# Rotary turn of the shared key by two row transfers and a column of signs in place of a product, and a planner that counts changes of the array's shape

## The chip, the core and the metric

The kernel runs on one core of a Trainium2 chip. A core has five engines with instruction streams of their own: TensorE (PE, the products, with a separate stream of weight loads, PEld), VectorE (DVE), ScalarE (ACT), GpSimd (POOL) and SyncE (SP, which here issues transfers). Streams wait for each other through semaphores only. The metric is the device time of one execution in microseconds (us), lower is better: the median of three executions before is 956.06 us (955.11 to 957.71).

## What is computed

One layer of a diffusion backbone over 512 latent tokens and 256 context tokens of 1024 features: modulated norms, then in parallel a latent attention with 16 heads and a two-way Mamba-2 scan with 16 heads, a joint output projection, and a gated MLP with a convolution on its gate. Cut to what the change touches, which is the rotary part of the key, shared by all heads:

```
cq_x, ckv_x, kr_x, z_x, xbc_x, dt_x = in_split(modulate(rms_norm(x, ...), ...) @ w_in)

def rotate_half_axial(x):                 # x: (..., 32)
    def rh(t):
        a, b = jnp.split(t, 2, axis=-1)
        return jnp.concatenate([-b, a], axis=-1)
    xr, xc = jnp.split(x, 2, axis=-1)
    return jnp.concatenate([rh(xr), rh(xc)], axis=-1)

def apply_rope(x, cos, sin):
    return x * cos + rotate_half_axial(x) * sin

k_rope_x = apply_rope(kr_x, cos, sin)     # 512 tokens x 32; context keys are not turned
s = (einsum("bqhd,bkhd->bhqk", q_nope, k_nope) + einsum("bqhr,bkr->bhqk", q_rope, k_rope)) * SCALE
```

The kernel holds the 32 features on partitions 32 to 63, reordered so that the two quarters a turn swaps are rows 32 to 47 and rows 48 to 63; the sine table is negative on rows below 64. Every product of weights and activations is made of rounded fp32r halves: a value is split into a high part (ACT copy, L597) and a low part (DVE subtraction, L598), and three products of halves replace one.

## The kernel before

The program is written once as plain code, and a planner then sets the order. build() (from L566) issues some 8,000 instructions in the order of the source. plan() collects them, prices each one (price), finds their dependences, and replays them on a model of the engines (Graph.schedule): each engine takes, of what is ready, the instruction of the lowest rank. refined() then changes ranks at random, with a fixed seed, 1200 times, and keeps a change that the model does not call longer. The orders that come out are the instruction streams. So a change of prices, of the rule for extra time (1340 ns in TABLE for each change of the ACT table) or of the instructions themselves makes the search draw another order for all engines.

Stages, by the profile's clock: modulation from 12 to 60 us, the input projections from there to about 245 us (products L862, 8 input blocks by three half products; the convolution on DVE L892, its smooth gate L903), with the key made on the way at L988; the scan's products; attention scores from 255 to 505 us; output projection; MLP with up projection to 840 us; and the down projection (L1671), which multiplies 2 by 2 blocks by a scheme with seven products, so that DVE makes sums of blocks (L1664, L1680, L1570) and splits them before a product can run.

Shared places set much of the waiting. The eight PSUM banks are cut into areas by hand: in the attention, two areas "sc" of 768 columns for score tiles and two banks "t" for transposed tiles. A score tile (L1309, six products) is reduced on DVE (L1311), exponentiated on ACT (L1313), which frees its area; the result is transposed by six products (L1325) into the two "t" banks, which ACT (L597) and DVE (L598) empty into halves. The weighted sums are L1337.

The rotary turn stands at L997 to L1003, behind the fused key product:

```
    pr = pget("b")
    mm(pr[:64, :S], lhsT=C("rot")[:64, :64], rhs=kd[:, :S], start=True, stop=True)
    kc, ks = t2(64, S), t2(64, S)
    V.tensor_tensor(out=kc[32:64], in0=kd[32:64, :S], in1=C("cos")[32:64], op=ALU.mult)
    V.tensor_tensor(out=ks[32:64], in0=pr[32:64, :S], in1=C("sin")[32:64], op=ALU.mult)
    pfree(pr)
    V.tensor_tensor(out=kd[32:64, :S], in0=kc[32:64], in1=ks[32:64], op=ALU.add)
```

The 64 by 64 matrix "rot" of zeros, ones and minus ones is a part of the constants that SP loads (L589, 64 KB); another transfer brings the tables "cos" and "sin" (512 KB). The product is plain fp32 and shows as two records. A changed line L997 of the new kernel is another one than L997 here: the new kernel's numbers are lower by 2 from L65 on, and by 3 from about L868 on.

Of the kernel before, what the change touches and what calls it, by code (L numbers as in the profile page):

```python
# [15 lines left out]
ALU = mybir.AluOpType  # L16
# [3 lines left out]
P = 128  # L20
# [26 lines left out]
_o = 0  # L47
for _n, _w in (("id", 128), ("sel", 32), ("rot", 128), ("trif", 128), ("trib", 128), ("cos", 512), ("sin", 512)):
    CST[_n] = (_o, _w)
    _o += _w  # L50
# [3 lines left out]
def constants():  # L54
    c = np.zeros((P, NCST), np.float32)

    def put(name, a):
        o, w = CST[name]
        c[: a.shape[0], o : o + w] = a

    i = np.arange(P)
    put("id", np.eye(P))
    put("trif", (i[:, None] <= i[None, :]))
    put("trib", (i[:, None] >= i[None, :]))
    rot = np.zeros((64, P))  # L65
    for m in range(16):
        rot[48 + m, 32 + m] = 1.0
        rot[32 + m, 48 + m] = -1.0
    put("rot", rot)
    t = np.arange(S)  # L70
    inv = np.float32(10000.0) ** (-np.arange(0, 16, 2, dtype=np.float32) / np.float32(16))
    ar = (t // GRID_W).astype(np.float32)[:, None] * inv
    ac = (t % GRID_W).astype(np.float32)[:, None] * inv
    ang = np.concatenate([ar, ac], -1).astype(np.float64)
    put("cos", np.tile(np.cos(ang).T, (8, 1)))
    put("sin", np.where(i[:, None] < 64, -1, 1) * np.tile(np.sin(ang).T, (8, 1)))
    put("sel", np.tile(np.eye(32), (2, 1)))
    return c
# [77 lines left out]

TABLE, TICK, WARM, BEGIN = 1340, 10240 / 3, 3060, 570


def price(x):  # L160
# [10 lines left out]
    if e == "PE":  # L171
        if ops[1][2].dtype == mybir.dt.float32r:
            return size(ops[1]) / (2.4 if size(ops[1]) >= 256 else 1.2) + (13 if ops[1][1][0][1] > 64 else 100)
        return max(107, size(ops[1]) / 1.2) if x.is_transpose else max(213, size(ops[1]) / 0.6)
# [35 lines left out]
def table(x):  # L210

    return {AF.Tanh: 0, AF.Exp: 0, AF.Ln: 1, AF.Gelu: 2, AF.Sqrt: 3}.get(getattr(x, "func", None))

# [99 lines left out]
class Graph:  # L313
# [39 lines left out]
    def schedule(self, rank, look=0.06, back=False):  # L353
# [7 lines left out]
        later, now, due = [[] for _ in ENGINES], [[] for _ in ENGINES], [never] * len(ENGINES)  # L361
        ticks, held, port, queue, flying = {}, 0, 0.0, 0.0, []
        push, pop = heapq.heappush, heapq.heappop
# [14 lines left out]
        for _ in range(n):  # L378
# [18 lines left out]
            c, d = cost[i], dma[i]  # L397
            if not back and tables[i] not in (None, held):
                held, t = tables[i], t + TABLE
            if shared[i]:  # L400
# [165 lines left out]
def build(nc, tc, ctx, a, out, dbg=None, places=None):  # L566
# [10 lines left out]
    def c_(shape, name, dt=F32):  # L577
        return cp.tile(list(shape), dt, name=name, tag=name, bufs=1)
# [9 lines left out]
    def load(dst, src, q=None):  # L588
        (q or nc.sync).dma_start(out=dst, in_=src)  # L589
# [68 lines left out]
    cs, csc = t4(), t4()  # L658
    cst = c_([P, P + 32 + P], "cst")
    prm = c_([P, NPRM], "prm")  # L660
    load(cst[:, : P + 32], a["cst"][:, : P + 32], nc.scalar)
    load(prm, a["prm"])
# [206 lines left out]

    load(cst[:, P + 32 :], a["cst"][:, P + 32 : 2 * P + 32])  # L870
    for name, w, get in (("trif", 256, t2), ("cos", 1024, t4)):
# [124 lines left out]

    pr = pget("b")  # L997
    mm(pr[:64, :S], lhsT=C("rot")[:64, :64], rhs=kd[:, :S], start=True, stop=True)
    kc, ks = t2(64, S), t2(64, S)
    V.tensor_tensor(out=kc[32:64], in0=kd[32:64, :S], in1=C("cos")[32:64], op=ALU.mult)  # L1000
    V.tensor_tensor(out=ks[32:64], in0=pr[32:64, :S], in1=C("sin")[32:64], op=ALU.mult)
    pfree(pr)
    V.tensor_tensor(out=kd[32:64, :S], in0=kc[32:64], in1=ks[32:64], op=ALU.add)  # L1003
# [848 lines left out]
```

## Time and profile before

| what | value |
|---|---|
| median of three executions | 956.06 us |
| profiled execution, its own time | 954.86 us |
| span of the profiled execution, first to last instruction | 953.1 us |
| granted TensorE clock, mean | 0.992 |
| score tiles: 64 reductions L1311 | 60.7 us of DVE |
| half splits: DVE L598, all forms | 461 instructions |

The profile is one execution. Its windows give, for a stretch of time, how long each engine was busy and with how many instructions; its waits give which instruction's end released an engine; its timeline gives starts and lengths one by one, neighbours of one kind together. The ends of products are modelled and they overlap, so what a product costs on TensorE is best read from the distance of starts. 954.86 us lies 1.20 us under the median and inside the range of the three.

### The profile page before, as it was taken

The page shows a single profiled execution, that of the slowest core. Times are in us where ns is not written, and L with a number is a line of the kernel's source. Part 1 is how long each engine was busy: PE and PEld are TensorE (multiplying, and loading weights), DVE is VectorE, ACT ScalarE, POOL GpSimd, SP SyncE. Part 2 cuts the span into 40 slices and gives each one's busy share as a digit, 9 for nine tenths or more (in the row PEclk, how much of TensorE's full clock was granted, in tenths as well). Part 3 has the DMA queues.
Part 4 walks back from the last instruction along what each step waited for, and adds up shares of the span by engine and source line. Part 5 has one row for each costly group of instructions (what it writes and reads, how often), then busy time and mean ns, then how long its engine had stood idle before and what let it go on. Part 6 is the DMA issues. An engine that isn't in the chain of part 4 may idle for free.

```text
span 953.1 us, 14651 instructions
## 1 busy us (share of the span) xinstructions
PE 938.1 (98%) x5116; PEld 802.4 (84%) x5116; DVE 749.7 (79%) x1378; ACT 526.1 (55%) x1038; POOL 246.2 (26%) x258
## 2 busy tenths in 40 slices
PE   8999999999999999999999999999999999999996
PEld 8888888888888988889898888988888888878785
DVE  6999868897989999877899986832544744579998
ACT  4465337544877878688895236633313322347674
POOL 0001001766669466522111100000000063240021
PEclk9999999999999999999999999999999999999999
DMA  9953103012432434244849874413343232856784
GB/s 346 335 179 127 50 1 100 1 51 78 103 67 62 114 101 110 55 104 99 253 168 326 277 245 153 177 67 133 133 177 132 89 111 69 206 112 196 235 286 145
DMA packets 54586, 137.52 MB, mean 144 GB/s; under 512 B 8033, under 2 KB 11121, under 8 KB 54513
## 3 DMA queue, kind: packets, MB, share of 16 engines
q1 hardware_dynamic: 52128, 132.03, 43.0%
q0 software_dynamic: 1584, 2.88, 1.9%
q10 hardware_dynamic: 800, 1.68, 0.6%
q8 instruction: 40, 0.66, 0.3%
q14 instruction: 34, 0.27, 0.1%
HBM read 114.50 MB, written 6.34 MB: 127 GB/s over the span
## 4 chain that ended last, share of the span: by engine, by line
PE 88%; DVE 7%; ACT 2%; issue 1%; DMA 1%; POOL 0%; SPq 0%; DVEq 0%; ACTq 0%
PE banks L862 43%; PE banks L1437 9%; PE banks L1309 6%; PE banks L1671 6%; PE banks L794 5%; PE banks L1337 4%; PE banks L1325 4%; DVE block L598 3%; PE banks L1235 2%; PE banks L1134 2%; DVE block L1664 1%; PE banks L706 1%; PE banks L1180 1%; PE banks L1172 1%; ACT block L597 1%
## 5 line engine op out<-in xcount | busy, mean ns | idle before, releaser
L862 PE MATMUL banks<-block,block 128*128 128x512 f32 (+1 forms) x2132 | 450.8, 362 | 0.4 <-DVE block L1258 0.3
L862 PEld LDWEIGHTS banks<-block,block 128*128 128x128 f32 x2132 | 359.4, 189 | 61.9 <-issue 1.6
L597 ACT ACTIVATE block<-block 128x512 fp32r<-128x512 f32 (+4 forms) x329 | 208.5, 670 | 150.7 <-DVE block L696 30.3
L598 DVE TENSOR_TENSOR block<-block,block 128x512 fp32r<-128x512 f32 (+3 forms) x305 | 236.3, 809 | 63.4 <-ACT block L597 34.4
L1671 PE MATMUL banks<-block,block 128*128 128x512 f32 x462 | 111.4, 396 | 2.8 <-DVE block L1680 2.1
L1671 PEld LDWEIGHTS banks<-block,block 128*128 128x128 f32 x462 | 87.1, 190 | 23.9 <-DVE block L1680 2.6
L1309 PE MATMUL banks<-block,block 128*128 128x512 f32 (+1 forms) x384 | 94.9, 352 | 0.2 <-ACT block L1313 0.2
L1437 PE MATMUL banks<-block,block 128*128 128x512 f32 x384 | 90.5, 391 | 0.0
L598 DVE TENSOR_TENSOR block<-banks,block 128x512 fp32r<-128x512 f32 (+1 forms) x156 | 83.2, 554 | 8.9 <-ACT block L597 8.5
L1437 PEld LDWEIGHTS banks<-block,block 128*128 128x128 f32 x384 | 71.4, 188 | 14.5 <-ACT block L1313 0.2
L597 ACT ACTIVATE block<-banks 128x256 fp32r<-128x256 f32 (+1 forms) x156 | 72.1, 496 | 20.1 <-PE banks L1325 13.6
L1337 PE MATMUL banks<-block,block 128*128 128x256 f32 x384 | 68.4, 294 | 0.2 <-DVE block L1370 0.2
L1311 DVE TENSOR_REDUCE smalls<-banks 128x1 f32<-128x768 f32 x64 | 60.7, 949 | 8.5 <-PE banks L1309 6.0
L1313 ACT ACTIVATE block<-banks,smalls 128x768 f32<-128x768 f32 x64 | 57.7, 901 | 16.4 <-DVE smalls L1311 15.4
L1309 PEld LDWEIGHTS banks<-block,block 128*128 128x128 f32 x384 | 60.0, 189 | 7.2 <-ACT block L1313 1.9
L696 DVE SCALAR_TENSOR_TENSOR block<-block,block 128x1024 f32<-128x1024 f32 x52 | 64.9, 1267 | 0.0
L1325 PE MATMUL banks<-cst,block 128*128 128x128 f32 x384 | 63.7, 273 | 0.4 <-DVE block L598 0.4
L892 DVE SCALAR_TENSOR_TENSOR block<-banks,cwh,block 128x510 f32<-128x510 f32 (+3 forms) x88 | 53.0, 621 | 9.7 <-ACT block L888 8.9
L1337 PEld LDWEIGHTS banks<-block,block 128*128 128x128 f32 x384 | 56.4, 189 | 4.2 <-ACT block L597 0.6
L1578 POOL TENSOR_TENSOR block<-block 128x256 f32<-128x256 f32 x11 | 10.2, 929 | 170.2 <-DVE block L1570 142.6
L1325 PEld LDWEIGHTS banks<-cst,block 128*128 128x128 f32 x384 | 46.7, 140 | 7.4 <-DVE block L598 2.0
L1564 ACT ACTIVATE block<-banks,prm 128x512 f32<-128x512 f32 x22 | 16.7, 776 | 61.0 <-PE banks L862 60.7
(244 smaller groups left out, 1115.5 us busy)
## 6 DMA issues: line engine op xcount, KB each, us to landing
block<-in_wmod_dram SPq DMA_DIRECT2D x48, 512.0 KB
block<-in_wup_dram SPq DMA_DIRECT2D x44, 512.0 KB
block<-in_wdn_dram SPq DMA_DIRECT2D x88, 256.0 KB
block<-block SPq DMA_DIRECT2D x32, 256.0 KB
block<-in_wout_dram SPq DMA_DIRECT2D x16, 512.0 KB
block<-in_wxbc_dram SPq DMA_DIRECT2D x12, 512.0 KB
block<-block SPq DMA_DIRECT2D x40, 128.0 KB
block<-in_wz_dram SPq DMA_DIRECT2D x16, 256.0 KB
```

The lines of the kernel that those rows point to most:

```text
L597: act(hi, src, AF.Copy)
L598: (lo_eng or V).tensor_tensor(out=lo, in0=src, in1=hi, op=ALU.subtract)
L696: V.scalar_tensor_tensor(out=junk, in0=wt, scalar=0.5, in1=vec, op0=ALU.mult, op1=ALU.mult, accum_out=acc)
L862: mm(po, lhsT=wf(k, pt[0]), rhs=xf(k, pt[1]), start=(k == 0 and pt == parts[0]), stop=(k == nk - 1 and pt == parts[-1]))
L892: V.scalar_tensor_tensor(out=st[:, lo:hi], in0=pm[:, lo + d : hi + d], scalar=cwh[:, m * 5 + j : m * 5 + j + 1], in1=st[:, lo:hi], op0=ALU ...
L1309: mm(sc[:, o : o + n], lhsT=q_[:, x_, qi * P : (qi + 1) * P], rhs=kk[:, y_, :], start=part == 0, stop=part == 2)
L1311: V.reduce_max(nm, sc[:, :T], axis=AX.X, negate=True)
L1313: act(pe, sc[:, :T], AF.Exp, bias=nm, scale=1.0, accum_out=sum_)
L1325: nc.tensor.transpose((tx if c < NX else tc_)[:, o : o + P], pe[:, s_ : s_ + P], ident)
L1337: mm(po[:, half * 256 : half * 256 + 256], lhsT=vst(c), rhs=rhs, start=(part == 0 and c == 0), stop=(part == 1 and c == NKT - 1))
L1437: mm(po[i][:, nh * 512 : nh * 512 + 512], lhsT=l[lp][:, i * P : (i + 1) * P], rhs=w[wp][:, nh * 512 : nh * 512 + 512], start=(k == 0 and l ...
L1671: mm(po[i], lhsT=l[:, lp, i * P : (i + 1) * P], rhs=w[wp], start=first and q == 0 and n == 0, stop=q == PAIRS[-1] and n == 2, skip_group_c ...
```

## The change

Three things. The product with "rot" goes, and its 64 KB of constants; a column "sign" of one number for each row takes its place in the first constants. Two transfers on SP's queue copy 16 rows each (32 KB) within on-chip memory, so that the rows stand swapped in a tile of their own, and DVE multiplies by sign and sine in one instruction that now reads no PSUM. The planner asks table() for PE too: the shape of the array in blocks of 32 rows and columns; every change of it adds TURN = 125 ns in the model. And price() charges fp32r products on few rows no longer 100 ns more, and halves those with 64 output rows.

```diff
-for _n, _w in (("id", 128), ("sel", 32), ("rot", 128), ("trif", 128), ...
+for _n, _w in (("id", 128), ("sel", 32), ("sign", 1), ("trif", 128), ...
...
-    rot = np.zeros((64, P))
-    for m in range(16):
-        rot[48 + m, 32 + m] = 1.0
-        rot[32 + m, 48 + m] = -1.0
-    put("rot", rot)
+    put("sign", np.where(i[:, None] < 48, 1, -1))
...
-TABLE, TICK, WARM, BEGIN = 1340, 10240 / 3, 3060, 570
+TABLE, TURN, TICK, WARM, BEGIN = 1340, 125, 10240 / 3, 3060, 570
...
-            return size(ops[1]) / (2.4 if size(ops[1]) >= 256 else 1.2) + (13 if ops[1][1][0][1] > 64 else 100)
+            return (size(ops[1]) / (2.4 if size(ops[1]) >= 256 else 1.2) + 13) / (2 if ops[0][1][0][1] == 64 else 1)
...
 def table(x):
+    if engine_of(x) == "PE":
+        return tuple(-(-v.bass_ap.ap[0][1] // 32) for v in (x.ins[0], x.outs[0]))
...
-        ticks, held, port, queue, flying = {}, 0, 0.0, 0.0, []
+        ticks, held, port, queue, flying = {}, [0 if e == "Activation" else (4, 4) for e in ENGINES], 0.0, 0.0, []
...
-            if not back and tables[i] not in (None, held):
-                held, t = tables[i], t + TABLE
+            if not back and tables[i] not in (None, held[e]):
+                held[e], t = tables[i], t + (TURN if e == PE else TABLE)
...
-    cst = c_([P, P + 32 + P], "cst")
+    cst = c_([P, P + 33], "cst")
-    load(cst[:, : P + 32], a["cst"][:, : P + 32], nc.scalar)
+    load(cst, a["cst"][:, : P + 33], nc.scalar)
...
-    load(cst[:, P + 32 :], a["cst"][:, P + 32 : 2 * P + 32])
...
-    pr = pget("b")
-    mm(pr[:64, :S], lhsT=C("rot")[:64, :64], rhs=kd[:, :S], start=True, stop=True)
     kc, ks = t2(64, S), t2(64, S)
+    load(ks[32:48], kd[48:64, :S])
+    load(ks[48:64], kd[32:48, :S])
     V.tensor_tensor(out=kc[32:64], in0=kd[32:64, :S], in1=C("cos")[32:64], op=ALU.mult)
-    V.tensor_tensor(out=ks[32:64], in0=pr[32:64, :S], in1=C("sin")[32:64], op=ALU.mult)
-    pfree(pr)
+    V.scalar_tensor_tensor(out=ks[32:64], in0=ks[32:64], scalar=C("sign")[32:64], in1=C("sin")[32:64], op0=ALU.mult,
+                           op1=ALU.mult)
     V.tensor_tensor(out=kd[32:64, :S], in0=kc[32:64], in1=ks[32:64], op=ALU.add)
```

Since the search draws anew, the streams differ nearly everywhere: PE's stand alike up to its 135th instruction. The multiset of work is the same but for the edit above. Three places, each written as line, operation, output and inputs, and size:

DVE behind the key, before. "block" names are tiles of the planned memory; block_109_662 is kd, block_131_748 the cosines and sines. Between these rows stand 94 others, then 52, then 2:

```order
L988 TENSOR_TENSOR block_109_662<-banks,block_70_471 64x768
...
L1000 TENSOR_TENSOR block_80_506<-block_109_662,block_131_748 32x512
...
L1001 TENSOR_TENSOR block_106_627<-banks,block_131_748 32x512
...
L1003 TENSOR_TENSOR block_109_662<-block_80_506,block_106_627 32x512
```

The same on DVE now; kd is block_20_227, the swapped rows block_58_427, the table block_7_85:

```order
L985 TENSOR_TENSOR block_20_227<-banks,block_120_696 64x768
...
L900 SCALAR_TENSOR_TENSOR block_71_473<-block_120_696,block_71_473 128x768
L596 TENSOR_TENSOR block_159_949<-block_87_526,block_159_949 128x512
L596 TENSOR_TENSOR block_153_889<-block_20_227,block_153_889 32x256
L997 TENSOR_TENSOR block_87_526<-block_20_227,block_7_85 32x512
L998 SCALAR_TENSOR_TENSOR block_58_427<-block_58_427,cst,block_7_85 32x512
L596 TENSOR_TENSOR block_205_1436<-block_70_471,block_205_1436 128x512
L1000 TENSOR_TENSOR block_20_227<-block_87_526,block_58_427 32x512
```

The three steps stood 95, 148 and 151 rows behind the key's row; now they stand 16, 17 and 19 rows behind it, among the first input projections. The two transfers stand on SP's queue thus, where gate_rows is a store of the gates of the scan (z) and in_wxbc_dram are weights of the projections:

```order
L587 DMA block_34_302<-in_wxbc_dram 128x1024
L587 DMA block_7_85<-in_cst_dram 128x1024
L587 DMA block_58_427<-block_20_227 16x512 x2
L587 DMA gate_rows<-block_80_506 128x512
L587 DMA block_34_302<-in_wxbc_dram 128x1024
L587 DMA block_80_506<-in_cst_dram 128x256
L587 DMA block_34_302<-in_wxbc_dram 128x1024
```

The table is loaded ahead of them, and what waits behind the two is one store and the weights of later projections. The second place is DVE at the entry of the down projection, before; block_159_952 is a left operand of the first products whose inputs come late:

```order
L1570 TENSOR_TENSOR block_1064_6793<-banks,block_1064_6793 128x512
L1570 TENSOR_TENSOR block_1088_6995<-banks,block_1088_6995 128x512
L598 TENSOR_TENSOR block_901_5509<-block_1176_7581,block_901_5509 128x512
L598 TENSOR_TENSOR block_1058_6726<-block_1166_7457,block_1058_6726 128x512
L598 TENSOR_TENSOR block_159_952<-block_195_1368,block_159_952 128x256
L1680 SCALAR_TENSOR_TENSOR block_159_952<-block_1140_7441,block_159_952 128x256
L598 TENSOR_TENSOR block_1011_6393<-block_987_6246,block_1011_6393 128x256
```

And the same entry now, with block_1029_6520 in that role:

```order
L1567 TENSOR_TENSOR block_1117_7243<-banks,block_1117_7243 128x512
L596 TENSOR_TENSOR block_159_949<-block_1175_7572,block_159_949 128x512
L596 TENSOR_TENSOR block_1029_6520<-block_978_6118,block_1029_6520 128x256
L1661 TENSOR_TENSOR block_1176_7580<-block_1064_6787,block_1146_7450 128x512
L1677 SCALAR_TENSOR_TENSOR block_1029_6520<-block_1140_7441,block_1029_6520 128x256
L596 TENSOR_TENSOR block_1090_6989<-block_1166_7456,block_1090_6989 128x512
L596 TENSOR_TENSOR block_901_5498<-block_1176_7580,block_901_5498 128x512
```

Two splits of 128x512 that stood ahead of the negated operand (now L1677) stand behind it, and a sum (now L1661) ahead. The third place is PE among the score tiles (L1309), transposes (L1325) and weighted sums (L1337), before:

```order
L1309 MATMUL banks<-block_714_4441,block_712_4440 128x512 x3
L1325 MATMUL banks<-cst,block_695_4339 128x128 x2
L1325 MATMUL banks<-cst,block_740_4628 128x128 x3
L1325 MATMUL banks<-cst,block_699_4371 128x128 x2
L1437 MATMUL banks<-block_797_5085,block_799_5088 128x512
L1337 MATMUL banks<-block_680_4200,block_676_4193 128x256 x3
L1309 MATMUL banks<-block_391_2534,block_712_4440 128x256 x3
```

And a stretch of the same kind now:

```order
L1306 MATMUL banks<-block_753_4700,block_550_3343 128x512 x2
L1322 MATMUL banks<-cst,block_783_4936 128x128 x2
L1334 MATMUL banks<-block_698_4356,block_160_952 128x256 x4
L1322 MATMUL banks<-cst,block_769_4807 128x128 x5
L1306 MATMUL banks<-block_715_4433,block_550_3343 128x256 x3
L1322 MATMUL banks<-cst,block_769_4807 128x128
L1334 MATMUL banks<-block_679_4192,block_153_889 128x256 x2
```

What stands between the score products of neighbouring tiles has changed: there transposes of three tiles and four other products, here more transposes of one tile and more weighted sums.

More of the change, by code (lines that the diff above doesn't have):

```diff
@@ L47 @@
 _o = 0
-for _n, _w in (("id", 128), ("sel", 32), ("rot", 128), ("trif", 128), ("trib", 128), ("cos", 512), ("sin", 512)):
+for _n, _w in (("id", 128), ("sel", 32), ("sign", 1), ("trif", 128), ("trib", 128), ("cos", 512), ("sin", 512)):
     CST[_n] = (_o, _w)
```

## The prediction

> **What bounds the kernel now.** I read the page's busy times first, then its chain of work that ended last, then the windows by stage, and last the waits of TensorE's weight loads.
>
> ```profile
> span 953.1 us, 14651 instructions
> PE 938.1 (98%) x5116; PEld 802.4 (84%) x5116; DVE 749.7 (79%) x1378; ACT 526.1 (55%) x1038; POOL 246.2 (26%) x258
> PE 88%; DVE 7%; ACT 2%; issue 1%; DMA 1%; POOL 0%; SPq 0%; DVEq 0%; ACTq 0%
> 100.00:155.00 55.00, 55.00 (x303) 46.95 (x302) 43.02 (x70) 23.05 (x36) 0.52 (x1) 1.00 0.15 44
> 155.00:245.00 90.00, 88.90 (x514) 76.23 (x514) 78.92 (x149) 49.33 (x98) 54.00 (x46) 0.98 0.21 61
> 300.00:400.00 100.00, 99.18 (x637) 86.56 (x636) 97.12 (x205) 78.43 (x183) 60.33 (x63) 1.00 0.39 95
> 400.00:505.00 105.00, 104.78 (x731) 94.24 (x730) 86.21 (x150) 90.31 (x193) 24.25 (x31) 1.00 0.54 156
> 840.00:900.00 60.00, 57.23 (x238) 44.90 (x237) 56.08 (x102) 38.03 (x82) 7.25 (x10) 0.97 0.58 172
> PEld banks L1671 <- DVE block L1680: 2.6, 1, 2.6
> PEld banks L1671 <- DVE block L598: 2.5, 6, 0.8
> PEld banks L1325 <- DVE block L598: 2.0, 5, 0.8
> PEld banks L1309 <- ACT block L1313: 1.9, 6, 0.4
> ```
>
> The first line is the span, the second the busy time of each engine, the third the shares of the chain by engine. The five lines of windows have the stretch, its length, then busy us (instructions) of PE, PEld, DVE, ACT and POOL, the granted clock, the DMA share and GB/s. The last four say which instruction of PEld waited for which, with us in all, times, and the longest. TensorE is busy 98 per cent and holds 88 per cent of the chain; in every window it is within 2.8 us of full. So work taken off TensorE shows one for one, and work on another engine shows only where TensorE waits for it: the four rows of waits, 9.0 us together, are most of what there is. In 300 to 400 us DVE has 2.88 us left of 100; in 100 to 155 us it has 12 of 55 left, and POOL is nearly still.
>
> **The product that goes.** These are TensorE's rows around it (start, length, instruction, count):
>
> ```profile
> 192.33 0.39 PE L1149 MATMUL banks<-block,sel 128*128 128x256 f32 x2
> 192.65 1.07 PE L998 MATMUL banks<-block,cst 64*64 64x512 f32 x2
> 193.65 1.09 PE L862 MATMUL banks<-block,block 128*128 128x256 f32 x5
> ```
>
> From its start to the next product's is 193.65 - 192.65 = 1.00 us. Its length, with the modelled end, is 1.07. Ahead of it the two L1149 take 0.32 us from start to start; if 0.1 of that belongs to the turn to a smaller array, 1.1 goes. I take **-1.0 us** (bounds -0.9, if neighbours fill the slot less tightly, to -1.1). It is in the second window, where TensorE misses 1.10 of 90 us, so the slot is on the path.
>
> **The rotary steps on DVE and SP.** Before, and where DVE stands idle in the first projections (the idle time ahead and its releaser in brackets):
>
> ```profile
> 102.08 0.94 DVE L988 TENSOR_TENSOR block<-banks,block 64x768 f32<-64x768 f32 x1
> 136.38 3.11 DVE L892 SCALAR_TENSOR_TENSOR block<-banks,cwh,block 128x510 f32<-128x510 f32 x4 [5.37 <-ACT block L888]
> 181.47 1.43 DVE L1000 TENSOR_TENSOR block<-block,block 32x512 f32<-32x512 f32 x1
> 206.50 0.68 DVE L1001 TENSOR_TENSOR block<-banks,block 32x512 f32<-32x512 f32 x1
> 209.23 0.68 DVE L1003 TENSOR_TENSOR block<-block,block 32x512 f32<-32x512 f32 x1
> ```
>
> The three steps are 1.43 + 0.68 + 0.68 = 2.79 us of DVE. They leave the window of 155 to 245 us and move to 16 to 19 rows behind the key's row (the order in the section on the change), which is some 13 us after 102.08. The new middle step reads three operands from on-chip memory; no row shows that form at this size, so I bound it by the rows of 32x512: 0.68 to 1.43. So DVE pays 2.0 to 3.5 us in a window where it has 12 to spare, with an idle stretch of 5.37 in it. On the path I put **0** (bounds 0 to +0.8, the excess of 1.43 over 0.68, if a convolution behind it is just then waited for). What covers it is L862's eight blocks of products ahead; without that cover it would be the whole 3.5.
>
> L1000's 1.43 us beside L1003's 0.68 is the same instruction at twice the time. The Trainium skill, page "SBUF — State Buffer", section "Who interferes with whom", says that a VectorE instruction with two inputs in on-chip memory contends with a GpSimd instruction that reads there, while one with at most one such input does not. That speaks against the edit, since L1001 read one input from PSUM and its successor reads both from on-chip memory. By it the step would cost up to 1.43 beside a busy POOL; but POOL is busy 0.52 of 55 us in the new place against 54.00 of 90 in the old one, so by the page the sum is the same, and the first step would even fall to 0.68. The trace agrees so far as one pair of rows can.
>
> The two transfers add two issues to SP, one goes. What is queued behind their wait for the key is one store and three loads. The weights among them feed projections two blocks on, and the split ahead of the products has slack there. How long a copy inside on-chip memory takes from issue to landing no row shows. The nearest rows:
>
> ```profile
> DMA to landing us min/median/max: 3.8/5.1/7.0
> POOL block L1378 <- DMA block<-sums: 60.1, 4, 26.8
> L598 DVE TENSOR_TENSOR block<-block,block 128x512 fp32r<-128x512 f32 (+3 forms) x305 | 236.3, 809 | 63.4 <-ACT block L597 34.4
> L892 DVE SCALAR_TENSOR_TENSOR block<-banks,cwh,block 128x510 f32<-128x510 f32 (+3 forms) x88 | 53.0, 621 | 9.7 <-ACT block L888 8.9
> ```
>
> The first is POOL's 256 KB loads of the down projection; the second a wait on a store and two loads behind it, 26.8 us at most. Between the key's row and the first rotary step DVE has 7 splits and 8 convolution steps (by the mean ns of the last two rows, behind the busy us, 7 x 0.809 + 8 x 0.621 = 10.6 us) and two more rows. Cover of 10.6 against 5.1 hides the transfers; against 26.8 DVE would stand 16 us, of which the 12 us of slack and the work ahead on TensorE take most. The value is the small one, **0** (bounds 0 to +4).
>
> **The planner.** Its new prices touch no product of this program: the few of a smaller array are 8 of 32 rows, 6 of 32 columns and the one that goes, and the first two kinds stand in a row in both orders. So the counting of shapes alone buys nothing; what it does is to draw a new order. I compared the two orders only at the waits that the trace shows.
>
> At the entry of the down projection TensorE runs 26 products, stands 2.14 us, then goes on:
>
> ```profile
> 841.35 6.08 PE L1671 MATMUL banks<-block,block 128*128 128x512 f32 x26
> 849.56 6.61 PE L1671 MATMUL banks<-block,block 128*128 128x512 f32 x21 [2.14 <-DVE block L1680]
> 844.67 4.50 DVE L598 TENSOR_TENSOR block<-block,block 128x512 fp32r<-128x512 f32 x3
> 849.09 0.41 DVE L1680 SCALAR_TENSOR_TENSOR block<-block,block 128x256 fp32r<-128x256 f32 x1
> 845.98 0.42 ACT L1679 ACTIVATE block<-block 128x256 fp32r<-128x256 f32 x1 [0.55 <-POOL block L1576]
> ```
>
> L1680 needs ACT's L1679, done at 846.40, but DVE ran three splits from 844.67 to 849.17 ahead of it. In the new order two of the three stand behind it and one sum of the same size ahead. So it can start one split earlier, 4.50 / 3 = 1.5, less what the sum takes and the split that TensorE asks for next. I take half of the wait, **-1.1** (bounds 0, if the next split is what is late then, to -2.1, all of it).
>
> Among the score tiles, an area is free again after reduction and exponential:
>
> ```profile
> L1311 DVE TENSOR_REDUCE smalls<-banks x64: 907/948/959, 255.8 to 498.3; 128x1 f32<-128x768 f32 x64
> L1313 ACT ACTIVATE block<-banks,smalls x64: 882/902/932, 256.8 to 499.4; 128x768 f32<-128x768 f32 x64
> 507.46 80.22 PE L1437 MATMUL banks<-block,block 128*128 128x512 f32 x353
> ```
>
> Their medians make 0.948 + 0.902 = 1.85 us and the hops between engines on top. The last row gives a product of 512 columns, 80.22 / 353 = 0.227 us. With that, and 0.11 to 0.12 for the narrow ones, the work that TensorE has between the last score product of one tile and the first of the second tile after it comes to under 3.0 us at 13 of 62 places in the old order and at one in the new. The wait for L1313 happened six times for 1.9 us. Most should go, but L1325's transposes stand right behind and wait for DVE themselves, so I take a third, **-0.6** (bounds 0 to -1.9).
>
> The sum: -1.0 - 1.1 - 0.6 = **-2.7 us**, 954.86 - 2.7 = 952.2 on the profiled execution's own time. That execution lies 1.20 under the median of 956.06, so against the runs it is **953.4**. A measurement of this kernel can tell about 0.3 per cent, 2.9 us, from no change: under 953.2 is faster, over 958.9 slower.
>
> **The rivals.**
> (a) Only the product shows: what the new order frees at two waits it gives back at others, since DVE's work is the same and full. 956.06 - 1.0 = 955.1. For it: the 9.0 us of the four rows are 18 waits at many places. Against it: nothing that I counted is worse at the entry.
> (b) The new order frees more than I counted: the four rows of waits lose two thirds of their 9.0 us, and the product goes: -6.0 - 1.0 gives 949.1. For it: waits at different tiles were drawn together. Against it: DVE at 97.12 of 100 us leaves little to shuffle.
> (c) Slower, by one mechanism: the transposes L1325 wait longer for their two banks, which two engines must empty.
>
> ```profile
> L598 DVE TENSOR_TENSOR block<-banks,block 128x512 fp32r<-128x512 f32 (+1 forms) x156 | 83.2, 554 | 8.9 <-ACT block L597 8.5
> L597 ACT ACTIVATE block<-banks 128x256 fp32r<-128x256 f32 (+1 forms) x156 | 72.1, 496 | 20.1 <-PE banks L1325 13.6
> ```
>
> Two copies and two subtractions, partly beside each other, make about 0.496 + 2 x 0.554 = 1.6 us, 2 with the hops. In the old order 15 of 63 tiles have their six transposes straight behind another tile's, in the new one 16, and what is missing to 2 us, summed over the tiles, grows from 61.1 to 66.6. TensorE paid 2.0 us at L1325 for the first, as DVE and ACT were ahead elsewhere; if the 5.5 come in full, 956.06 - 1.0 + 5.5 = 960.6. It decides from 3.9 us of new waits on, where the product's 1.0 no longer holds it under 958.9. For it: DVE's 97 per cent in 300 to 400 us. Against it: it paid a thirtieth of the shortfall before.
> (d) The change doesn't do what it says, in its second half: no product's price moved and there is no series of shape changes to save. That is true by the count above and already in the sum.
>
> **How the numbers follow.** The forecast 0.48, about evenly on both sides of 953.2 (its own range 950.5 to 955.5, by the bounds of its terms); (a) 0.15; (b) 0.15; (c), with late transfers, 0.22. Faster: 0.25 + 0.15 = 0.40; within 0.3 per cent: 0.23 + 0.15 = 0.38; slower 0.22. The range goes from (b) at 949.0 to (c) at 960.6.
>
> **What would show it.** Right: no record of a 64*64 product; TensorE's busy time lower by about 1; the middle step at 0.68 near 115 us, with no wait of SP's landing on DVE over 1 us; the wait of L1671's successor for the negated operand near 1; the row of waits of the score products on the exponential under 1.3. Wrong: a row in which transposes wait for the splits over 4 us, or a projection's split late behind SP. What makes the sum wrong is a wait that I did not compare: the orders differ from the 135th product on, and I read three places.

## The result and the profile after

The changed kernel takes 948.64 us (median of eight, 947.15 to 949.43) beside 955.54 us of the kernel before in the same comparison (eight, 950.34 to 957.71): ratio 0.9934, 95% interval 0.991 to 0.9957. By this ratio it is 6.3 us faster, between 4.1 and 8.6; the two medians lie 6.9 us apart. The prediction had the sign and a gain of 2.7. The profiled execution took 947.64 us, 7.2 less than the one before. Its page, first the span, then busy time by engine, then the chain by engine:

```profile
span 945.9 us, 14643 instructions
PE 930.0 (98%) x5114; PEld 798.0 (84%) x5114; DVE 752.8 (80%) x1378; ACT 529.5 (56%) x1038; POOL 248.7 (26%) x258
PE 89%; DVE 4%; DMA 3%; issue 1%; ACT 1%; POOL 0%; SPq 0%; DVEq 0%; ACTq 0%; POOLq 0%
```

TensorE has two records fewer and 8.1 us less of busy time, far more than one product; "busy" also holds stretches in which products run at half clock (shown below) and the modelled ends of products. The windows after, in the columns of before:

```profile
155.00:245.00 90.00, 90.00 (x540) 79.37 (x539) 82.94 (x156) 54.34 (x108) 61.12 (x53) 1.00 0.22 63
300.00:400.00 100.00, 99.94 (x643) 88.08 (x642) 94.40 (x198) 80.24 (x186) 60.79 (x66) 1.00 0.40 101
400.00:505.00 105.00, 102.83 (x714) 92.23 (x713) 89.68 (x159) 88.19 (x185) 18.43 (x22) 1.00 0.57 166
840.00:900.00 60.00, 58.30 (x251) 46.00 (x250) 57.53 (x112) 40.98 (x90) 2.39 (x4) 1.00 0.64 196
```

In 155 to 245 us TensorE now does 540 products where it did 514. That is more than the 1.10 us of idle time there before can explain: within "busy" the products stand closer. So I counted, over all products of both traces, by how much the distance of one start to the next exceeds the usual one of its width (0.227 us for 512 columns, 0.120 for 256, 0.109 for 128), and summed it by stage, in us:

| stretch, us | before | after |
|---|---|---|
| 0 to 60 | 5.7 | 4.0 |
| 60 to 155 | 1.3 | 0.9 |
| 155 to 245 | 5.5 | 1.0 |
| 245 to 300 | 1.1 | 3.1 |
| 300 to 400 | 4.3 | 2.2 |
| 400 to 505 | 3.1 | 5.0 |
| 505 to 840 | 1.0 | 1.2 |
| 840 to the end | 6.2 | 4.2 |

The columns sum to 28.2 and 21.6; with the 0.5 us that the two records of the removed product are worth by the same widths, that is 7.1 of the 7.2 us. The gain is in the scan's stage (4.5), in 300 to 400 us (2.1), at the end (2.0) and ahead of 60 us (1.7), and 3.9 us are given back around the scores. What lies ahead of 60 us is no doing of the change. The clock that was granted from 12 to 60 us, before and then after, is the third number from the end:

```profile
12.00:60.00 48.00, 48.00 (x280) 42.62 (x281) 43.30 (x104) 23.34 (x39) 0.00 (x0) 0.96 0.91 331
```

```profile
12.00:60.00 48.00, 48.00 (x285) 42.31 (x285) 45.15 (x104) 25.21 (x42) 0.00 (x0) 1.00 0.89 333
```

0.04 of 48 us is 1.9 us. turn_fixed, a kernel below that runs in the order of before, was granted 1.00 there too, and in six of the seven other executions of the changed kernel the mean clock over the whole span is 0.995 or 0.996 where this one has 0.999. So single executions differ by this much whatever the kernel, and the table compares one execution with one. The rotary steps after, VectorE's first, then the issue of the two transfers on SP's queue:

```profile
100.85 0.94 DVE L985 TENSOR_TENSOR block<-banks,block 64x768 f32<-64x768 f32 x1
...
114.21 0.68 DVE L997 TENSOR_TENSOR block<-block,block 32x512 f32<-32x512 f32 x1
114.81 0.73 DVE L998 SCALAR_TENSOR_TENSOR block<-block,cst,block 32x512 f32<-32x512 f32 x1
...
116.30 0.68 DVE L1000 TENSOR_TENSOR block<-block,block 32x512 f32<-32x512 f32 x1
```

```profile
107.12 1.24 SPq L587 DMA_DIRECT2D block<-block  x2
```

The three steps take 0.68 + 0.73 + 0.68 = 2.09 us. No idle time stands ahead of L998, so both transfers had landed at the latest 6.5 us after both were issued (114.81 less 108.36, the end of the row). And the waits of TensorE's weight loads after, in the place of the four rows of before:

```profile
PEld banks L1322 <- DVE block L596: 5.1, 10, 2.4
PEld banks L1668 <- DVE block L596: 4.7, 9, 1.0
PEld banks L1306 <- ACT block L1310: 1.1, 4, 0.4
```

The score products' wait fell from 1.9 to 1.1 us, that of the transposes rose from 2.0 to 5.1, 2.4 of it in one place. The three rows make 10.9 us where the four of before made 9.0. At the entry of the down projection:

```profile
837.82 4.69 PE L1668 MATMUL banks<-block,block 128*128 128x512 f32 x20
843.06 9.18 PE L1668 MATMUL banks<-block,block 128*128 128x512 f32 x39 [0.55 <-DVE block L596]
```

The 2.14 us there are 0.55 now.

### The profile page after: what moved, and what is told of

Read it like the earlier page. It is cut to its first block, busy times and chain, and to the rows that moved or that the text cites. A ratio compares the mean times of both kernels' runs of the same rounds, so it can differ in the third digit from the quotient of the medians.

```text
span 945.9 us, 14643 instructions
## 1 busy us (share of the span) xinstructions
PE 930.0 (98%) x5114; PEld 798.0 (84%) x5114; DVE 752.8 (80%) x1378; ACT 529.5 (56%) x1038; POOL 248.7 (26%) x258
## 4 chain that ended last, share of the span: by engine, by line
PE 89%; DVE 4%; DMA 3%; issue 1%; ACT 1%; POOL 0%; SPq 0%; DVEq 0%; ACTq 0%; POOLq 0%
PE banks L860 44%; PE banks L1434 9%; PE banks L1668 8%; PE banks L1306 6%; PE banks L792 5%; PE banks L1322 4%; PE banks L1334 4%; PE banks L1232 2%; DVE block L596 2%; PE banks L1177 1%; PE banks L1169 1%; PE banks L1131 1%; DMA block<-block 1%; PE banks L704 1%; DMA block<-in_wdn_dram 1%
## 5 line engine op out<-in xcount | busy, mean ns | idle before, releaser
L595 ACT ACTIVATE block<-block 128x512 fp32r<-128x512 f32 (+5 forms) x329 | 210.1, 670 | 129.0 <-DVE block L694 21.1
L596 DVE TENSOR_TENSOR block<-block,block 128x512 fp32r<-128x512 f32 (+4 forms) x305 | 237.8, 813 | 50.6 <-PE banks L860 25.8
L1306 PE MATMUL banks<-block,block 128*128 128x512 f32 (+1 forms) x384 | 99.0, 354 | 0.0
L595 ACT ACTIVATE block<-banks 128x512 fp32r<-128x512 f32 (+1 forms) x156 | 73.9, 495 | 19.8 <-PE banks L1322 13.1
L1334 PE MATMUL banks<-block,block 128*128 128x256 f32 x384 | 72.3, 296 | 0.0
L1322 PE MATMUL banks<-cst,block 128*128 128x128 f32 x384 | 67.9, 274 | 2.6 <-DVE block L596 2.5
L1306 PEld LDWEIGHTS banks<-block,block 128*128 128x128 f32 x384 | 61.5, 189 | 6.8 <-ACT block L1310 1.1
L1334 PEld LDWEIGHTS banks<-block,block 128*128 128x128 f32 x384 | 57.5, 189 | 4.0 <-DVE block L596 0.3
L889 DVE SCALAR_TENSOR_TENSOR block<-banks,cwh,block 128x511 f32<-128x511 f32 (+3 forms) x88 | 53.6, 620 | 7.9 <-ACT block L885 7.0
L1322 PEld LDWEIGHTS banks<-cst,block 128*128 128x128 f32 x384 | 47.3, 141 | 10.2 <-DVE block L596 5.1
```

Of the source, the lines that this page charges most:

```text
L595: act(hi, src, AF.Copy)
L596: (lo_eng or V).tensor_tensor(out=lo, in0=src, in1=hi, op=ALU.subtract)
L889: V.scalar_tensor_tensor(out=st[:, lo:hi], in0=pm[:, lo + d : hi + d], scalar=cwh[:, m * 5 + j : m * 5 + j + 1], in1=st[:, lo:hi], op0=ALU ...
L1306: mm(sc[:, o : o + n], lhsT=q_[:, x_, qi * P : (qi + 1) * P], rhs=kk[:, y_, :], start=part == 0, stop=part == 2)
L1322: nc.tensor.transpose((tx if c < NX else tc_)[:, o : o + P], pe[:, s_ : s_ + P], ident)
L1334: mm(po[:, half * 256 : half * 256 + 256], lhsT=vst(c), rhs=rhs, start=(part == 0 and c == 0), stop=(part == 1 and c == NKT - 1))
```

## The experiments

**Three theories.** First, that of the prediction: the product is worth its slot of 1.0 us, the rest is the newly drawn order. Second: the rotary edit is worth most of the gain, since with the product goes the bank of PSUM in which its result waited for VectorE, from 192.65 us to the end of L1001 at 207.18, one of two that the projections' transposes (L907) use. Third: the planner's count of shapes does it. A side question was whether TensorE's longer waits cost more than their own length.

**The product alone, in the old order (turn_fixed).** The plan is made for the program of before, and the program that is built then differs from it at the product, the two transfers and the step that reads what they bring:

```diff
-    mm(pr[:64, :S], lhsT=C("rot")[:64, :64], rhs=kd[:, :S], start=True, stop=True)
+    if places is None:                      # while planning
+        mm(pr[:64, :S], lhsT=C("rot")[:64, :64], rhs=kd[:, :S], start=True, stop=True)
     kc, ks = t2(64, S), t2(64, S)
+    if places is not None:                  # while building
+        load(ks[32:48], kd[48:64, :S])
+        load(ks[48:64], kd[32:48, :S])
...
+    order["PE"].remove(1202)                # the product; SP's two loads behind that of the tables
```

> The order of before held fixed on every engine; only the product with rot is left out, the two transfers stand on SP's queue behind the load of the tables, and the second rotary step reads the turned rows. The theory of the prediction (the product is worth its 1.0 us, the rest of the gain is the new order): 1.0 us faster than before, ratio 0.999, and waits as in before. The rival (the rotary edit itself is worth most of the gain, since it frees a bank of PSUM): 4 us or more faster even in the old order, if no instruction has to be moved for that; about 1 us if the bank counts only where the planner can use it.

Measured: 955.62 us beside 955.72, ratio 0.9995 (0.9977 to 1.0013). The product is gone and nothing is gained that can be measured. TensorE's timeline at the old place (line numbers are higher by 9 there, L1158 is L1149 of before):

```profile
191.44 0.99 PE L863 MATMUL banks<-block,block 128*128 128x256 f32 x5
193.11 0.83 PE L1158 MATMUL banks<-block,sel 128*128 128x256 f32 x4 [0.68 <-DVE block L1166]
```

Where the product stood for 1.00 us, TensorE now stands for VectorE's predicated copy. By the count above this wait is 0.85 us over the usual distance. From the pair of L1149 ahead of the product to the row of L862 that starts at 195.05 us, the order of before took 2.72 us with the product and takes 2.57 without it: 0.15 of the slot is left as a gain. What bears on it is the window of 177 to 212 us, of before, of turn_fixed and of the changed kernel:

```profile
177.00:212.00 35.00, 35.00 (x200) 29.49 (x198) 34.63 (x69) 16.04 (x35) 23.65 (x22) 1.00 0.06 19
```

```profile
177.00:212.00 35.00, 34.24 (x200) 29.14 (x199) 34.65 (x67) 16.21 (x34) 24.26 (x21) 1.00 0.08 23
```

```profile
177.00:212.00 35.00, 35.00 (x216) 31.14 (x214) 33.21 (x65) 18.03 (x36) 26.25 (x24) 1.00 0.15 44
```

VectorE is busy 34.63 of 35 us there before, and TensorE gets through 200 products with the one for the turn among them and 200 without: around the product TensorE stands for a VectorE that runs without a gap, and the product had covered this wait. In the new order VectorE has 1.4 us less to do in this window and TensorE does 216.

**The rotary edit alone, the planner's part alone (rot_only, plan_only), and other seeds of the random search (rot_s4, before_s4).** rot_only is the changed kernel with the planner's three hunks taken back, plan_only the kernel before with these hunks; in the other two the search starts from another number:

```diff
-        chance = random.Random(3)
+        chance = random.Random(4)
```

> The rotary edit alone, planned by the old planner without the count of shapes: a new order is drawn. If the gain is that of the rotary edit (product, and the bank of PSUM that it held while DVE was busy elsewhere): as the changed kernel, about 948 to 950. If the gain is luck of the drawn order: anywhere between 948 and 956, and no nearer to the changed kernel than to the one before. If it is the planner's count of shapes: about 954 to 955.

> The planner's part alone, with the product kept: a new order is drawn. If the gain is that of the rotary edit: 953 to 957, as before. If it is the planner's count: 949 to 951. If it is luck of the drawn order: anywhere between 948 and 957.

> The kernel before with another seed of the planner's random search, nothing else. If what the drawn order is worth is small beside the rotary edit: 953 to 957. If the drawn order alone moves the time by as much as the change did: below 950.5 or above 960.

> The rotary edit alone with the old planner and another seed. If the rotary edit carries the gain: 947.5 to 950.5, whatever the seed. If the drawn order does: anywhere between 947 and 956.

| kernel | product | ratio to before, 95% |
|---|---|---|
| changed | no | 0.9934 (0.991 to 0.9957) |
| rot_only | no | 0.9927 (0.9907 to 0.9947) |
| rot_s4 | no | 0.9971 (0.9954 to 0.9988) |
| plan_only | yes | 0.9962 (0.9946 to 0.9978) |
| before | yes | 1 |
| before_s4 | yes | 1.0034 (1.0018 to 1.005) |

The planner's part is not needed for the gain. But an order drawn anew is worth something by itself: plan_only, in which no price moves, is 3.6 us faster, before_s4 3.2 us slower. Means of three are 0.9944 without the product and 0.9999 with it, 5.3 us apart; the slowest without the product and the fastest with it lie the other way round. Three orders of each kind, which scatter over 4 us without the product and 7 us with it, suggest that the edit itself is worth a part of this, but are too few to show it. In 155 to 245 us the two kinds do not overlap, though plan_only comes close; the windows of rot_only, rot_s4, plan_only and before_s4 in this order:

```profile
155.00:245.00 90.00, 90.00 (x536) 78.95 (x535) 84.28 (x160) 55.03 (x107) 58.53 (x49) 1.00 0.24 66
```

```profile
155.00:245.00 90.00, 90.00 (x534) 78.38 (x533) 80.27 (x157) 54.19 (x106) 57.64 (x49) 1.00 0.24 68
```

```profile
155.00:245.00 90.00, 89.95 (x531) 77.97 (x530) 83.76 (x155) 53.65 (x108) 56.85 (x49) 1.00 0.22 60
```

```profile
155.00:245.00 90.00, 88.15 (x507) 75.38 (x507) 81.70 (x148) 49.41 (x97) 52.34 (x46) 0.98 0.21 60
```

540, 536 and 534 products without the product with rot; 531, 514 and 507 with it. By the count over starts the stage loses 1.0 (changed), 0.8 and 1.2 us without it, and 2.6 (plan_only), 5.5 (before) and 6.7 us with it. plan_only also speaks against the second theory: it has the product and its bank in the middle of this stage,

```profile
184.75 1.07 PE L1000 MATMUL banks<-block,cst 64*64 64x512 f32 x2
```

```profile
202.21 0.68 DVE L1003 TENSOR_TENSOR block<-banks,block 32x512 f32<-32x512 f32 x1
```

so from 184.75 to 202.89 us the bank is held 18.1 us, longer than the 14.5 of before, and still its stage loses less than half as much.

**The bank put back (turn_b).** The changed kernel, its first rotary product of VectorE written to a bank "b":

```diff
-    kc, ks = t2(64, S), t2(64, S)
+    pr = pget("b")
+    kc, ks = pr[:64, :S], t2(64, S)
...
     V.tensor_tensor(out=kd[32:64, :S], in0=kc[32:64], in1=ks[32:64], op=ALU.add)
+    pfree(pr)
```

> The changed kernel, but the product of key and cosine is written to one of the two banks of PSUM that the old product used, and the bank is held until the sum, as the old product's bank was held until DVE read it; no product of TensorE, no other work added. If the bank is what the edit freed: back at 954 to 958, 5 to 9 us slower than the changed kernel. If the bank is worth nothing: 948 to 951, since TensorE's work is the same and only a new order is drawn.

Measured: 964.0 us, ratio 1.009 (1.0067 to 1.0112): slower than before, and 15 us over the changed kernel, more than twice what the orders of either kind in the table spread. Its window of the stage, and the two steps between which the bank is held:

```profile
155.00:245.00 90.00, 86.78 (x502) 74.48 (x501) 81.22 (x147) 48.28 (x95) 55.55 (x46) 0.98 0.16 48
```

```profile
174.11 0.82 DVE L998 TENSOR_TENSOR banks<-block,block 32x512 f32<-32x512 f32 x1
...
199.27 0.68 DVE L1001 TENSOR_TENSOR block<-banks,block 32x512 f32<-32x512 f32 x1
```

Here the bank is held from 174.11 to 199.95, 25.8 us, where the kernel before held it 14.5. TensorE does 502 products in the window, the fewest of all. But not all of the loss sits there: by the count over starts turn_b's profiled execution, its slowest (969.07 us), loses 7.1 us more than the changed kernel's in 155 to 245 us, 6.4 more in 300 to 400 and 4.3 more behind 840, where the turn holds no bank. So this order with a bank of "b" held is a bad one, also without any product on TensorE; how much of that is the bank is not shown, and how much of the old kernel's loss its 14.5 us were is not told by this.

**The place of the rotary steps (turn_late, prod_early, turn_less).** turn_late is the changed kernel, replanned, with the steps held behind the fifth projection's last VectorE instruction; prod_early is the kernel before with its seven lines of the turn moved in the source to straight behind the key; turn_less is turn_fixed with the two multiplications left out as well, so that its key is not the turned one:

```diff
+    holds.append(((began, late), (late, here())))     # turn_late
...
-    for m in (8, 0, 1, 2, 3):                         # prod_early: these two lines behind the turn
-        xbc(m)
...
+    order["DVE"] = [i for i in order["DVE"] if i not in (1203, 1204)]   # turn_less
```

> The changed kernel, replanned, with its three rotary steps on VectorE held behind the convolution of the fifth projection, near 168 us, where the kernel before had them; no product, no bank. If the gain is the place of the steps (out of the stretch that VectorE paces): 952 to 955. If it is the product and its bank of PSUM: 948 to 950, as the changed kernel.

> The kernel before, but the product and the rotary steps are written straight behind the key in the source, so that they may run near 110 us with the bank taken there and freed there; the product stays. If the gain of the change is the early place: 949 to 951 (the product's slot is still paid). If a bank taken in the first projections costs there as much as it does later, or if the draw decides: 953 to 958.

> The order of before held fixed, the product left out, and the two multiplications by cosine and sine (L1000, L1001) left out too: the turned rows are added to the key as they are. VectorE has 2.1 us less to do between 181 and 207 us, TensorE 1.0 us less. Theory (in 155 to 245 us VectorE sets the pace, which is why leaving out the product alone brought nothing): 1 to 2.5 us faster than before, and the new wait of 0.85 us at L1149 shrinks. Rival (the stage is held by something else): within 0.7 us of before, as with the product alone.

Measured: turn_late 951.27 us, ratio 0.9973 (0.9955 to 0.9992); prod_early 957.64 us, 1.0037 (1.002 to 1.0053); turn_less 953.27 us, 0.9986 (0.9974 to 0.9999). The first two missed their mark as tests of the place. In turn_late the first step and in prod_early the product came at

```profile
148.84 0.68 DVE L999 TENSOR_TENSOR block<-block,block 32x512 f32<-32x512 f32 x1
```

```profile
149.82 1.07 PE L992 MATMUL banks<-block,cst 64*64 64x512 f32 x2
```

so ahead of the stretch and not in it. What they do say: an early product doesn't bring the gain, for prod_early is slower than before, though with the bank given back at 152.3 us its scan stage loses only 2.6 us, as plan_only's does; by the same count it loses 2.2 us more than before in 300 to 400. And turn_late, whose steps come 34 us later than the changed kernel's, still loses only 1.4 us in 155 to 245 us; its 0.39 per cent over the changed kernel lie in 300 to 505 us, 11.8 against 7.2 us, and are within what a seed does. turn_late also bears on the bank: it holds none, yet its transposes, which need both banks "b", stop at 165 us and go on at 204.5, much as those of before do from 167.8 to 208.8. So in before they would not have run much earlier with the bank free, unless the planner had ordered other work ahead. turn_less took 2.1 us of VectorE's work out of the stretch and gained 1.3 us (0.1 to 2.5) over before, barely told apart from turn_fixed, though the stage loses 5.6 us by the count where turn_fixed loses 6.5; the wait at L1149 stayed, 0.80 us by the count above, against what I expected. Where the first of the two steps had run, VectorE now stands:

```profile
182.34 0.75 DVE L892 SCALAR_TENSOR_TENSOR block<-banks,cwh,block 128x510 f32<-128x510 f32 x1 [1.25 <-ACT block L888]
```

So 1.25 of the 1.43 us of that step went into a wait for ScalarE, whose L888 had itself stood 3.77 us for TensorE's products L862. TensorE and VectorE wait for each other in this stage, neither alone sets its pace, and the two steps are a part of the gain at most.

**The entry of the down projection (wait_down).** In the order of before, GpSimd's sums L1577 to L1579 of one block are made to wait for L1680:

```diff
+        behind = mybir.DependencyInfo(mybir.DependencyClass.Sync, mybir.DependencyReason.DATA)
+        tc.add_manual_dep(real[6961], real[7083].name, behind, reason="POOL behind DVE")
```

> The order of before, with one wait more: GpSimd's second to fourth sum of the block whose negative TensorE waits for (L1577 to L1579) start only when VectorE has done that negation (L1680), so that they no longer run beside the split ahead of it, which took 2.75 us there where its kind takes 0.41. Theory: the split falls to 0.41, L1680 comes about 2 us earlier, TensorE's wait of 2.14 us at the entry of the down projection goes, and with it the half clock that follows it in some executions (8 products of 0.43 us in place of 0.23, 1.6 us): 2.1 to 3.9 us faster, 952 to 953.5. Rival (the next split is late then, or the sums are missed later): less than 0.7 us.

Measured: 951.53 us, ratio 0.9972 (0.9957 to 0.9986), 2.7 us faster. VectorE and TensorE there, in the new trace:

```profile
847.09 2.16 DVE L598 TENSOR_TENSOR block<-block,block 128x512 fp32r<-128x512 f32 x3
849.18 0.41 DVE L1680 SCALAR_TENSOR_TENSOR block<-block,block 128x256 fp32r<-128x256 f32 x1
```

```profile
843.76 12.54 PE L1671 MATMUL banks<-block,block 128*128 128x512 f32 x54
```

The three splits, 4.50 us before, take 2.16, and TensorE's 54 products run on without a wait. Before, GpSimd's sums started at 846.50, 847.21 and 847.89, and the third split ran from 846.42 to 849.17. The Trainium skill, page "SBUF — State Buffer", section "Who interferes with whom", says that a VectorE instruction with two inputs in on-chip memory, as the split has, contends with a GpSimd one that reads there. The trace agrees: the split took 2.75 us beside the sums. It also shows that the wait can last over several GpSimd instructions in a row.

**TensorE's wait for the sums over rows (wait_scan).** In the order of before, seven products go ahead of L944:

```diff
+    pe = planned[2]["PE"]
+    at = pe.index(1716)
+    pe[at : at + 13] = pe[at + 6 : at + 13] + pe[at : at + 6]
```

> The order of before, but seven products L862 that stood behind the sums over rows of the key and value projection (L944) stand ahead of them, so that TensorE does not stand for GpSimd's L941 near 222 us. Theory: the wait of 1.1 us goes, and with it the half clock that follows it in some executions (8 products, 1.6 us): 1.1 to 2.7 us faster, 953 to 954.6. Rival (VectorE sets the pace of this stage, and TensorE only waits elsewhere, as it did where the product was left out): within 0.5 us of before.

Measured: 953.07 us, ratio 0.9996 (0.998 to 1.0011). A wait is still there, one product later and for another of GpSimd's results:

```profile
225.45 1.67 PE L862 MATMUL banks<-block,block 128*128 128x512 f32 x6 [1.71 <-POOL block L598]
```

The split that GpSimd makes for these products was late as well, so at this place filling one wait uncovered the next.

**One exchange in the changed kernel (after_swap).** On ScalarE a split that waits for a transfer stands behind the exponential and the copy that were queued behind it:

```diff
+    o = planned[2]["Activation"]
+    at = o.index(4778)
+    o[at : at + 3] = o[at + 2], o[at + 1], o[at]
```

> The changed kernel with one exchange in ScalarE's order near 465 us: a split of 128x1024, which stood there 3.07 us for a transfer, stands behind the exponential and the copy out of a transpose bank that were queued behind it and were ready. Theory: TensorE's wait of 2.2 us for that bank goes: 1.5 to 2.3 us faster than the changed kernel, 946 to 947.5. Rival (the split's result is late then, or VectorE is): within 0.5 us of the changed kernel.

Measured: 948.63 us, ratio to before 0.9943 (0.9921 to 0.9964): the changed kernel's time. The wait at the transposes shrank, and another took its place:

```profile
467.48 0.44 PE L1322 MATMUL banks<-cst,block 128*128 128x128 f32 x2 [0.65 <-DVE block L596]
```

```profile
PEld banks L1334 <- DVE block L1367: 2.0, 1, 2.0
```

TensorE's 2.17 us at L1322 became 0.65, and the 2.0 us of its weight loads at L1334 are new; TensorE itself stands 1.5 us there. No version tried is faster than the changed kernel beyond its interval.

## Why the prediction was right and wrong

**The sign was right, the sum was too small**: 2.7 us where 6.3 were measured. Off the 956.06 of the prediction this is 949.8, under the forecast's own range of 950.5 to 955.5 and next to rival (b)'s 949.1, but that is luck: by (b) the four rows of waits lose two thirds of their 9.0 us, and after the change three of them alone make 10.9. The range was also not what the bounds give: they add up to 951.0 at the low end and, with the late transfers, to 960.0 at the high end.

**The product's 1.0 us.** The step that failed is "work taken off TensorE shows one for one", and with it "so the slot is on the path". turn_fixed shows 0.5 us, and its interval, from 2.2 us faster to 1.2 slower, holds 0 and 1.0 alike; it is its trace that decides, with the wait that took all but 0.15 us of the slot. I had read a stage in which TensorE is busy 98 per cent as one that TensorE bounds. My own window of that stage was too long: over 90 us VectorE shows 78.92 and seems to have room; over the 35 us around the product it has 0.37.

**What I didn't price at all: the scan's stage in the new order, and the bank.** I followed the product, the transfers and VectorE's steps, and noted nothing of the bank in which the product's result waited 14.5 us, nor of TensorE's other waits in this stage. In the planned order the drop of product and bank goes with 534 to 540 products in 155 to 245 us where there were 507 to 531, and with 5.3 us as a mean over three orders each. Which part of the edit does this stays open, since every kernel that changes it draws a new order. turn_b speaks for the bank, plan_only and turn_late speak against it. The rotary steps that moved out of the stretch are the other candidate; turn_less, which takes 2.1 us of them away in the old order, is 1.3 us faster than before. What the traces do show is where the 4.5 us of the stage were lost before: 1.13 us at one wait, L944's for GpSimd's L941, and 1.6 at the half clock behind it (below), neither of which the changed kernel has; the rest is spread.

**The rotary steps and transfers.** The mechanism was right: steps at 114 to 117 us, 0.73 us for the new one at the foot of the 0.68 to 1.43 that I gave, no wait for a landing, cover enough.

**The planner.** Rightly said to move no price and to work only through the drawn order; plan_only's 3.6 us and before_s4's 3.2 the other way show how large that is. A drawn order is a term with a spread of 3 us and more on either side, larger than each term of my sum, and I gave it none of its own.

**The entry.** The place and the sign were right, the term mis-sized: -1.1 against 1.6 of the 2.14 us in this trace, and 2.7 us when wait_down removes it alone. My reading of its cause was wrong. I took three splits of 1.5 us each; they were 0.67, 1.22 and 2.75, the last the smallest of the three and held up by GpSimd. In the new order GpSimd's sums run from 837.6 to 841.5 us, and now it is the negated operand's own step that runs beside them:

```profile
839.07 2.73 DVE L1677 SCALAR_TENSOR_TENSOR block<-block,block 128x256 fp32r<-128x256 f32 x1
```

It took 0.41 us before. TensorE has products in store there, up to 842.51 us by its row in the section on the result, so only the wait of 0.55 us shows.

**The scores.** -0.6 was about right for L1306 (1.9 to 1.1), but the rival (c) came in part: 3.1 us of new waits at the transposes. In 400 to 505 us the count went from 3.1 to 5.0. after_swap shows that taking the largest of these waits away brings nothing.

**Half clock.** The eight products behind the wait of 2.14 us took 3.45 us in the trace before, 0.43 us each on average in place of 0.227; turn_fixed has the same wait and the products behind it are at full speed:

```profile
848.84 7.33 PE L1680 MATMUL banks<-block,block 128*128 128x512 f32 x31 [2.14 <-DVE block L1689]
```

31 in 7.33 us against 21 in 6.61. The 1.13 us ahead of L944 are followed by eight such products too, from 224.79 to 228.18 us. So a wait of 1 to 2 us is followed by some 3.4 us at half clock (8 x 0.43) in some executions and not in others, and costs up to 1.6 us more; of the scan's 4.5 us and of the end's 2.0 in the table 1.6 each are of this kind. The Trainium skill, page "TensorE: Matmul & The Clock Gate", section "Part 1: The HAM clock gate (the "warmup" mystery)", has a free-running window of about 3.4 us by which activity is judged. The trace agrees in the length, and a window that runs freely would make the one execution pay and the other not. It differs in the cause, for the section has the clock fall only after an idle window of that length, and here 2.14 and 1.13 us went ahead of it. Waits of this kind may be behind the spread of the executions too, 950.34 to 957.71 us before and 947.15 to 949.43 after; that was not tested.

## What to carry to other kernels

A small product that leaves an engine's queue takes with it what it held and the order that it imposed on others, so list the bank and the buffer beside its own duration, and don't take the first of them that fits for the cause: here the kernel that held the bank longer than before lost less. A stage in which the busiest engine is at 98 per cent may still be paced by others that feed it. A sign is that another engine runs without gaps there; leaving the work out in a fixed order, and looking at what wait takes its place, tells what the work is worth in that order. Where a random search sets the order, run two or three seeds of both kernels before a gain of half a per cent is put down to an edit.

## What was not expected of the hardware

Three sums of GpSimd in a row held up one short VectorE instruction for 2.3 us, 2.75 in place of 0.41. A wait of TensorE of only 1.13 us was followed, in the trace before and 2.1 us after its end, by eight products at half speed: those behind L944, at 0.43 us each.
